# Moving one of two running sums of the first layer's modulation from VectorE to ScalarE and GpSimd

## The chip, the cores and the metric

The kernel runs on one core of a Trainium2 chip. The metric is the device time of one execution in microseconds (us), lower is better. Engines are called as in the profile: PE (TensorE matmul), PEld (its weight load), DVE (VectorE), ACT (ScalarE), POOL (GpSimd), SP (SyncE, which issues most of the DMAs).

## What is computed

The reference is a two-layer transformer block stack in fp32 on 256 tokens `x` and 256 context tokens `ctx`, width 1024. Each layer begins with a modulation that is made from two conditioning vectors, one for `x` and one for `ctx`:

```
mod_x = silu(c)     @ w_mod[l] + b_mod[l]     # 6 x 1024 columns
mod_c = silu(c_ctx) @ w_mod[l] + b_mod[l]
sh1, sc1, g1, sh2, sc2, g2 = split(mod, 6)
h = rmsnorm(x) * (1 + sc1) + sh1;   x = x + g1 * token_mixer(h)
h = rmsnorm(x) * (1 + sc2) + sh2;   x = x + g2 * channel_mixer(h)
```

The token mixer is a Fourier mix beside a gated linear attention; the channel mixer is a SwiGLU in layer 0 and eight experts with top-2 routing in layer 1. In layer 0 both token sets are carried, so each modulation is needed twice.

## The kernel before

fp32 products are made from high and low parts: a weight unit of 128x1024 is loaded on SP's queue (`load_unit`, L128), ACT writes its rounded high part (L145), DVE subtracts to get the low part (L149), and PE adds three products (`mm3`, L156 to L158). A unit's four `raw` places, three `hi` and three `lo` places come free when its readers are done. Stages follow one another: first modulation on PE, mixer of layer 0 (about 30 to 205 us), its output projection (to about 265 us), SwiGLU (to about 645 us), mixer of layer 1, experts.

The first two of the six modulation parts are made on PE at the start. The other four, for layer 0 (`g_mod(0, 1, 2)`, `s_mod(0, 1, 2)`, `g_mod(0, 2, 2)`), and all that follow for layer 1, run as side work in the function `mod_chunk` (L402): 512 columns at a time. A chunk has four loads of 256 rows of `w_mod` into a ring of three places (L128, `ring="mraw"`), and for each of its eight blocks of 128 rows one DVE instruction per conditioning vector (L419): `acc[x] = w * cs[x] + acc[x]`, 128x512 fp32. `x` is 0 for `c` and 1 for `c_ctx`. Each `acc` is first zeroed on POOL (L409) and gets `b_mod` in its first row by a small DMA on ACT's queue (L410). At the end of a chunk PE sums over the partitions with a matrix of ones: as rows (L425, copied by ACT, L426) or as columns (L429, copied by DVE, L431). The columns become `ac` (L360), which the normalised tokens are scaled by (L305 to L310).

A planner puts the instructions of each engine in order ahead of the run, by priority; every engine and every DMA queue then works strictly in that order. The L419 instructions stand inside `with later(LATER)`, which puts their priority 250 steps back: they fill room that the planner saw on DVE. The loads, the PE sums and the zeroing are not put back. Side work is pulled on by the main loops, one step for one or two weight units (`pull(mods, 1)`).

In the mixer DVE also runs the gated attention's levels (`widen`, L579 to L584, and the masked copies L642); the score matmuls (L598) and the PE sums L425 and L429 take their PSUM banks from one ring of four, tag `sc`.

Of the kernel before, what the change touches and what calls it, by code (L numbers as in the profile page):

```python
# [15 lines left out]
AF = mybir.ActivationFunctionType  # L16
OP = mybir.AluOpType
# [54 lines left out]
def hybrid_kernel(ctx: ExitStack, tc: tile.TileContext, a: dict, out: bass.AP, dbg=None, upto="end"):  # L72
    nc = tc.nc
# [18 lines left out]
    def spot(i, n=1):  # L92
        return spots[i // 4][:, i % 4:i % 4 + n, :].rearrange("p a b -> p (a b)")
# [27 lines left out]
    def load_unit(src, shape, ring="raw", queue=None):  # L121
        n = shape[0] * shape[1]
        if ring == "mraw":
            raw = spot(2 * (turn["mraw"] % 3), 2)[:, :n]
            turn["mraw"] += 1
        else:
            raw = place_of("raw", n)
        ins = (queue or nc.sync).dma_start(raw.rearrange("p (a b) -> p a b", a=shape[0]), src).ins  # L128
        if queue:
            return raw, shape  # L130
        behind(ins, W.get("load"))
        W["unit"] = ins
        if chained():
            W["load"] = ins
        return raw, shape
# [16 lines left out]
    def wsrc(w2d, r0, nb, c0, cols):  # L152
        return w2d[r0:r0 + nb * 128, c0:c0 + cols].rearrange("(k p) c -> p k c", p=128)
# [75 lines left out]
    cs = consts.tile([128, 16], F32, name="cs")  # L229
# [7 lines left out]
    def small(shape):  # L237
        return ps0.tile([128, 512], F32, name="sc", tag="sc", bufs=4)
# [164 lines left out]
    def mod_chunk(l, col, n_src, rows_out=None, cols_out=None):  # L403


        accs = []
        for x in range(n_src):
            acc = spot(10 + x)
            nc.gpsimd.memset(acc, 0.0)  # L409
            nc.scalar.dma_start(acc[0:1, :], a["b_mod"][l:l + 1, col:col + 512])  # L410
            accs.append(acc)
        for q in range(4):
            raw, _ = load_unit(wsrc(a["w_mod"][l], q * 256, 2, col, 512), (2, 512), ring="mraw")
            rv = raw.rearrange("p (a b) -> p a b", a=2)
            for k in range(2):
                kb = q * 2 + k
                for x in range(n_src):
                    with later(LATER):
                        nc.vector.scalar_tensor_tensor(accs[x], rv[:, k, :], cs[:, x * 8 + kb:x * 8 + kb + 1],  # L419
                                                       accs[x], op0=OP.mult, op1=OP.add)  # L420
            yield
        for x in range(n_src):
            ps = small([128, 512])
            if rows_out is not None:
                nc.tensor.matmul(ps, ones, accs[x], start=True, stop=True)  # L425
                nc.scalar.activation(rows_out[x], ps, AF.Copy)  # L426
            else:
                for j in range(4):
                    nc.tensor.matmul(ps[:, j:j + 1], accs[x][:, j * 128:(j + 1) * 128], ones[:, 0:1],  # L429
                                     start=True, stop=True)  # L430
                nc.vector.tensor_copy(cols_out[x], ps[:, 0:4])  # L431
# [3 lines left out]
    def g_mod(l, which, n_src):  # L435
        col = (2 if which == 1 else 5) * D
        if (l, which) == (1, 2):

            for hh in range(2):
                yield from mod_chunk(l, col + hh * 512, n_src, cols_out=[gcol[:, hh * 4:(hh + 1) * 4]])  # L440
            return
        gp[l, which] = [hbp.tile([128, D], F32, name="g", tag="g1", bufs=1) if l else spot(6 + 2 * x, 2)
                        for x in range(n_src)]
        for hh in range(2):
            yield from mod_chunk(l, col + hh * 512, n_src,
                                 rows_out=[g[:, hh * 512:(hh + 1) * 512] for g in gp[l, which]])

    def s_mod(l, which, n_src):
        mc = modp.tile([128, 2, 16], F32, name="modc", tag="modc", bufs=2)
        modc[l, which] = mc  # L450
        for ch in range(4):
            yield from mod_chunk(l, (0 if which == 0 else 3) * D + ch * 512, n_src,
                                 cols_out=[mc[:, x, ch * 4:(ch + 1) * 4] for x in range(n_src)])
# [845 lines left out]
    for turn_ in range(2):  # L1299
        for eng in range(2):  # L1300
            for j in range(4):
                k4 = turn_ ^ eng
                kb = 4 * k4 + j
# [507 lines left out]
```

## Time and profile before

| | us |
|---|---|
| median of 3 runs | 1665.8 |
| lowest, highest | 1665.4, 1669.24 |
| the profiled execution | 1667.27 |
| its span, first to last instruction | 1665.5 |

The profiled execution's time is 1.77 us above its span and 1.5 us above the median of the runs. In the profile, a row of a timeline or of the chain of waits begins with the start and the length in us; a group row gives a line, an engine, an operation, what is written and read, the count, the busy time and the mean length in ns. Rows that merge several instructions count them as x2, x3.

### The profile page before, as it was taken

To read this page: it belongs to the slowest core of one execution; us is meant where nothing else is said; L and a number is where in the kernel's file an instruction comes from. 1 tells how busy PE (TensorE), PEld (TensorE's weight loads), DVE (VectorE), ACT (ScalarE), POOL (GpSimd) and SP (SyncE) were. 2 spreads that over 40 slices of the span, in tenths; PEclk is the share of its full clock that TensorE was granted. 3 is DMA by queue.
4 is the path that set the end of the run, shared out by engine and by line. 5 is a ranking of instruction groups with operands and counts; after the bars stand their busy time and mean duration, and the time that the engine had idled before them with its cause. 6 is when DMAs were issued, how large, how long until landed. Compare 5 with 4: busy or idle time off the path is not lost.

```text
span 1665.5 us, 21562 instructions
## 1 busy us (share of the span) xinstructions
PE 1606.3 (96%) x8150; PEld 1159.5 (70%) x8150; DVE 1046.6 (63%) x1314; ACT 726.1 (44%) x892; POOL 27.5 (2%) x54
## 2 busy tenths in 40 slices
PE   7989999999999999999999999999999999999995
PEld 3868888788888888877786357874478844578532
DVE  3798897888567656866995127862178820588322
ACT  4733455322321347554775036741267611567201
POOL 1000000000000000000000000000000000000000
PEclk9999999999999999999999999999999999999997
DMA  9534385565666544546999999999999999999995
GB/s 372 160 102 136 96 267 163 163 189 171 189 190 201 156 128 140 174 154 240 332 357 318 415 406 413 407 406 407 409 412 409 410 390 408 410 414 406 384 405 201
DMA packets 186586, 479.06 MB, mean 288 GB/s; under 512 B 11585, under 2 KB 64961, under 8 KB 171873
## 3 DMA queue, kind: packets, MB, share of 16 engines
q1 hardware_dynamic: 185040, 473.80, 77.1%
q10 hardware_dynamic: 1074, 2.72, 0.5%
q8 instruction: 68, 1.11, 0.3%
q0 software_dynamic: 352, 1.00, 0.2%
q14 instruction: 52, 0.43, 0.1%
HBM read 476.43 MB, written 1.05 MB: 287 GB/s over the span
## 4 chain that ended last, share of the span: by engine, by line
PE 83%; DMA 6%; DVE 6%; ACT 3%; issue 1%; SPq 1%; DVEq 0%; ACTq 0%
PE h L1591 11%; PE mm L156 8%; PE mm L157 8%; PE mm L158 8%; PE h L1600 6%; PE h L1603 6%; PE h L1599 6%; PE y L156 5%; PE y L157 5%; PE y L158 5%; PE y L1623 4%; DMA rr<-moe_w 3%; PE sc L598 1%; PE sc L1570 1%; DVE lo L149 1%
## 5 line engine op out<-in xcount | busy, mean ns | idle before, releaser
L145 ACT ACTIVATE hi<-raw 128x1024 fp32r<-128x1024 f32 x127 | 134.6, 1059 | 303.2 <-PE mm L157 100.3
L177 DVE TENSOR_TENSOR rb<-raw,rb 128x2048 fp32r<-128x2048 f32 x73 | 167.1, 2290 | 80.2 <-ACT rb L177 60.5
L149 DVE TENSOR_TENSOR lo<-raw,hi 128x1024 fp32r<-128x1024 f32 x127 | 155.2, 1223 | 80.3 <-ACT hi L145 78.9
L419 DVE SCALAR_TENSOR_TENSOR rr<-rr,cs,rr 128x512 f32<-128x512 f32 x256 | 181.9, 747 | 9.6 <-DMA rr<-b_mod 4.6
L1600 PE MATMUL h<-rb,hg 128*128 128x512 f32 x448 | 177.2, 396 | 4.5 <-DVE rb L177 4.4
L156 PE MATMUL mm<-hbk,hi 128*128 128x512 f32 (+1 forms) x456 | 166.5, 366 | 1.1 <-DVE tm L837 1.0
L157 PE MATMUL mm<-hbk,hi 128*128 128x512 f32 (+1 forms) x456 | 163.6, 359 | 0.5 <-DVE hbk L310 0.5
L158 PE MATMUL mm<-hbk,lo 128*128 128x512 f32 (+1 forms) x456 | 163.8, 359 | 0.0
L177 ACT ACTIVATE rb<-raw 128x2048 fp32r<-128x2048 f32 x73 | 139.9, 1917 | 51.0 <-PE h L1603 31.8
L1591 PE MATMUL h<-raw,hgs 128*64 128x512 f32 (+1 forms) x720 | 143.4, 528 | 0.0
L177 DVE TENSOR_TENSOR sil<-sil,h 128x512 f32<-128x512 f32 (+1 forms) x44 | 29.1, 662 | 165.7 <-PE h L1591 148.5
L1599 PE MATMUL h<-rb,hg 128*128 128x512 f32 x288 | 109.1, 399 | 1.4 <-ACT rb L177 1.4
L1591 PEld LDWEIGHTS h<-raw,hgs 128*64 128x64 f32 x720 | 51.6, 137 | 77.5 <-issue 69.3
L1600 PEld LDWEIGHTS h<-rb,hg 128*128 128x128 f32 x448 | 85.1, 190 | 26.7 <-DVE rb L177 6.9
L177 DVE TENSOR_TENSOR rb<-raw,part 128x2048 fp32r<-128x2048 f32 x42 | 96.1, 2288 | 10.1 <-PE h L1600 4.6
L156 PEld LDWEIGHTS mm<-hbk,hi 128*128 128x128 f32 x456 | 85.9, 189 | 16.6 <-issue 2.7
L177 DVE TENSOR_TENSOR rb<-rr,rb 128x2048 fp32r<-128x2048 f32 x35 | 80.0, 2288 | 27.7 <-ACT rb L177 24.1
L177 ACT ACTIVATE part<-raw 128x2048 fp32r<-128x2048 f32 x42 | 80.4, 1914 | 36.2 <-DMA raw<-moe_w 16.8
L157 PEld LDWEIGHTS mm<-hbk,hi 128*128 128x128 f32 x456 | 86.0, 189 | 14.1 <-issue 1.0
L158 PEld LDWEIGHTS mm<-hbk,lo 128*128 128x128 f32 x456 | 86.0, 189 | 13.0
L1603 PE MATMUL h<-rb,hg 128*128 128x512 f32 x288 | 88.6, 393 | 2.5 <-DVE hg L177 2.5
L157 PE MATMUL y<-rb,ht 128*128 128x512 f32 x224 | 87.6, 391 | 0.0
(381 smaller groups left out, 2967.9 us busy)
## 6 DMA issues: line engine op xcount, KB each, us to landing
raw<-moe_w SPq DMA_DIRECT2D x212, 1024.0 KB
rr<-moe_w SPq DMA_DIRECT2D x110, 1024.0 KB
rr<-w_mod SPq DMA_DIRECT2D x80, 512.0 KB
raw<-ffn_w SPq DMA_DIRECT2D x72, 512.0 KB
raw<-w_in SPq DMA_DIRECT2D x32, 512.0 KB
raw<-w_out SPq DMA_DIRECT2D x23, 512.0 KB
raw<-moe_w SPq DMA_DIRECT2D x12, 512.0 KB
rb<-w_mod SPq DMA_DIRECT2D x5, 1024.0 KB
```

What stands on the lines that cost most here:

```text
L145: ins = nc.scalar.activation(hi, raw, AF.Copy).ins
L149: nc.vector.tensor_tensor(lo, raw, hi.bitcast(F32), op=OP.subtract)
L156: nc.tensor.matmul(ps, lh, rh, start=start, stop=False)
L157: nc.tensor.matmul(ps, lh, rl, start=False, stop=False)
L158: nc.tensor.matmul(ps, ll, rh, start=False, stop=stop)
L177: r = getattr(self.engine, name)(*args, **kw)
L419: nc.vector.scalar_tensor_tensor(accs[x], rv[:, k, :], cs[:, x * 8 + kb:x * 8 + kb + 1], accs[x], op0=OP.mult, op1=OP.add)
L1591: nc.tensor.matmul(H[i][0][x * 64:x * 64 + 64, :n], HG[e][:, k0 + j, :], hi[:, j, x * n:(x + 1) * n], start=(k0 + j == 0), stop=(k0 + j == 7))
L1599: nc.tensor.matmul(H[i][b], hgh[:, kb, :], hi[:, j, bc], start=(kb == 0), stop=False)
L1600: nc.tensor.matmul(H[i][b], hgh[:, kb, :], lo[:, j, bc], start=False, stop=False)
L1603: nc.tensor.matmul(H[i][b], hgl[:, kb, :], hi[:, j, bc], start=False, stop=(kb == 7))
L1623: nc.tensor.matmul(Y[e][0][hh * 64:hh * 64 + 64], ht[:, j0 + j, half], hi[:, j, xc], start=on, stop=off)
```

## The change

In layer 0's chunks of `mod_chunk`, the sum for `x = 1` is made in two steps on other engines: ACT multiplies the weight block in place by the column `cs` (an ACTIVATE Copy with a scale), and POOL adds it to the sum. The sum for `x = 0` stays on DVE, and so do all sums of layer 1. Both new instructions are under the same `later(LATER)`.

```diff
@@ -415,9 +415,14 @@
             for k in range(2):
                 kb = q * 2 + k
                 for x in range(n_src):
+                    c_ = cs[:, x * 8 + kb:x * 8 + kb + 1]
                     with later(LATER):
-                        nc.vector.scalar_tensor_tensor(accs[x], rv[:, k, :], cs[:, x * 8 + kb:x * 8 + kb + 1],
-                                                       accs[x], op0=OP.mult, op1=OP.add)
+                        if x and l == 0:
+
+                            nc.scalar.activation(rv[:, k, :], rv[:, k, :], AF.Copy, scale=c_)
+                            nc.gpsimd.tensor_tensor(accs[x], accs[x], rv[:, k, :], op=OP.add)
+                        else:
+                            nc.vector.scalar_tensor_tensor(accs[x], rv[:, k, :], c_, accs[x], op0=OP.mult, op1=OP.add)
             yield
         for x in range(n_src):
             ps = small([128, 512])
```

## Rows read from the trace of the kernel before

**Rows 1.** The page: span, busy time by engine, the span in 40 slices.
```profile
span 1665.5 us, 21562 instructions
PE 1606.3 (96%) x8150; PEld 1159.5 (70%) x8150; DVE 1046.6 (63%) x1314; ACT 726.1 (44%) x892; POOL 27.5 (2%) x54
...
PE   7989999999999999999999999999999999999995
...
DMA  9534385565666544546999999999999999999995
```

**Rows 2.** Stages of 25 us: busy time of each engine, with the sum.
```profile
100.00:125.00 25.00, 20.64 (x153) 16.34 (x152) 24.97 (x42) 8.25 (x13) 0.00 (x0) 1.00 0.44 128
125.00:150.00 25.00, 25.00 (x163) 19.73 (x162) 24.23 (x42) 11.53 (x14) 1.05 (x2) 1.00 0.34 105
...
250.00:275.00 25.00, 23.40 (x177) 21.94 (x176) 23.95 (x49) 15.58 (x34) 0.00 (x0) 1.00 0.54 156
275.00:300.00 25.00, 25.00 (x110) 20.06 (x110) 13.42 (x18) 9.24 (x14) 1.05 (x2) 1.00 0.49 139
...
sum 275.00, PE 268.30 PEld 220.88 DVE 232.28 ACT 129.07 POOL 9.78; mean PE 24.39 PEld 20.08 DVE 21.12 ACT 11.73 POOL 0.89
```

**Rows 3.** The chain of waits, 93 to 125 us: start, length, what.
```profile
101.28 1.36 DVE rr L419 x3
...
110.54 0.73 DVE rr L419 x2
...
121.28 3.41 issue
124.70 1.96 PE sc L425 x4
```

**Rows 4.** DVE in order of time, places where the sums run.
```profile
43.72 0.75 DVE L419 SCALAR_TENSOR_TENSOR rr<-rr,cs,rr 128x512 f32<-128x512 f32 x1
...
101.16 2.73 DVE L419 SCALAR_TENSOR_TENSOR rr<-rr,cs,rr 128x512 f32<-128x512 f32 x4
...
110.42 2.07 DVE L419 SCALAR_TENSOR_TENSOR rr<-rr,cs,rr 128x512 f32<-128x512 f32 x3
...
118.78 2.84 DVE L419 SCALAR_TENSOR_TENSOR rr<-rr,cs,rr 128x512 f32<-128x512 f32 x4
...
123.87 0.72 DVE L642 COPY_PREDICATED A<-masks,sc 128x512 f32<-128x512 uint8 x1
...
263.14 3.40 DVE L419 SCALAR_TENSOR_TENSOR rr<-rr,cs,rr 128x512 f32<-128x512 f32 x5
```

**Rows 5.** POOL's groups, whole span.
```profile
L409 POOL MEMSET rr<- 128x512 f32 x32 | 16.8, 525 | 536.2 <-PE mm L425 98.5 <-DVE sil L1029 98.1 <-PE mm L429 80.4
...
L1731 POOL TENSOR_TENSOR res<-macc,raw 128x512 f32<-128x512 f32 x2 | 2.5, 1271 | 893.2 <-DVE macc L177 892.5 <-DVE rn L267 0.7
```

**Rows 6.** POOL's copies at L471 (minimum, median, maximum ns), and DVE beside them.
```profile
L471 POOL COPY rr<-rr x8: 290/294/846, 27.9 to 580.4; 128x128 f32<-128x128 f32 x8
...
27.92 1.00 POOL L471 COPY rr<-rr 128x128 f32<-128x128 f32 x4 [11.48 <-DMA rr<-w_in]
...
577.94 2.32 DVE L419 SCALAR_TENSOR_TENSOR rr<-rr,cs,rr 128x512 f32<-128x512 f32 x3
...
578.51 2.14 POOL L471 COPY rr<-rr 128x128 f32<-128x128 f32 x4 [7.69 <-issue]
```

**Rows 7.** DVE's groups from 100 to 150 us.
```profile
L419 DVE SCALAR_TENSOR_TENSOR rr<-rr,cs,rr 128x512 f32<-128x512 f32 x25 | 17.2, 745 | 0.1
L642 DVE COPY_PREDICATED A<-masks,sc 128x512 f32<-128x512 uint8 x22 | 16.0, 732 | 0.0
```

**Rows 8.** ACT, an SBUF to SBUF copy of 128x512 at L475.
```profile
L475 ACT ACTIVATE rr<-rr x2: 614/624/633, 580.3 to 580.9; 128x512 fp32r<-128x512 f32 x2
```

**Rows 9.** DVE in order of time, the last sum of four later chunks.
```profile
152.26 1.41 DVE L419 SCALAR_TENSOR_TENSOR rr<-rr,cs,rr 128x512 f32<-128x512 f32 x2
...
175.79 0.74 DVE L419 SCALAR_TENSOR_TENSOR rr<-rr,cs,rr 128x512 f32<-128x512 f32 x1
...
205.79 0.74 DVE L419 SCALAR_TENSOR_TENSOR rr<-rr,cs,rr 128x512 f32<-128x512 f32 x1
...
236.85 0.75 DVE L419 SCALAR_TENSOR_TENSOR rr<-rr,cs,rr 128x512 f32<-128x512 f32 x1
```

**Rows 10.** The chain of waits around the PE sums of the same four chunks.
```profile
154.16 1.68 PE sc L429 x16
...
177.76 1.68 PE sc L429 x16
...
207.21 0.79 PE sc L429 x8
...
238.86 0.79 PE sc L429 x8
```

**Rows 11.** Who waited for whom: SP's queue from 20 to 330 us, then ACT up to 700 us.
```profile
SPq L128 <- DVE rr L419: 116.9, 30, 13.4
...
ACT hi L145 <- PE mm L157: 100.3, 29, 4.8
...
ACT hi L145 <- DMA raw<-ffn_w: 4.1, 1, 4.1
```

**Rows 12.** The page: DVE's groups for weight splits and attention levels, L419 among them.
```profile
L149 DVE TENSOR_TENSOR lo<-raw,hi 128x1024 fp32r<-128x1024 f32 x127 | 155.2, 1223 | 80.3 <-ACT hi L145 78.9
L419 DVE SCALAR_TENSOR_TENSOR rr<-rr,cs,rr 128x512 f32<-128x512 f32 x256 | 181.9, 747 | 9.6 <-DMA rr<-b_mod 4.6
```

## The prediction

> **What bounds the kernel now.** I read the page first: PE is busy in 1606.3 of 1665.5 us and DVE in 63% [rows 1]. That is an average, so I went to the stages in which nearly all of the changed instructions run, from 50 to 325 us, cut in pieces of 25 us. There PE is busy for 268.30 of 275 us [rows 2], so it waits 6.70 us. This is the first thing to see: whatever DVE is spared, PE can't get back more than those 6.70 us, and some 0.7 us before 50 us, because PE's own work does not change. The second thing is where they lie: 4.36 us (25.00 - 20.64) between 100 and 125 us, where DVE is busy for 24.97 of 25 us, and 1.60 us between 250 and 275 us, where DVE has 23.95 [rows 2]. From 275 to 300 us DVE has 13.42 and PE does not wait at all [rows 2]: there a lighter DVE is worth nothing. The chain of waits agrees: through the first of these places it runs on DVE, L419 in it, and then shows 3.41 us before the PE sum L425 [rows 3]. What lies behind 325 us is full of PE and, in its second half, of DMA [rows 1]; it begins when the stages before it end, so I pass a gain or a loss on to the end one to one.
>
> **The change, part by part.** Layer 0 has eight chunks here (two, four and two of `g_mod`, `s_mod`, `g_mod`) with eight blocks each: 64 L419 leave DVE, 64 ACT copies and 64 POOL additions come.
>
> *What DVE is spared.* Four L419 in a row take 2.73 us, three take 2.07 us [rows 4]: 0.66 us more for each one more. So DVE is spared 64 x 0.66 = 42 us, nearly all beside PE work that goes on anyway. On the path I count three places. Between 101 and 122 us there are 4 + 3 + 4 = 11 L419 [rows 4]; half of them are for x = 1, so the L642 that ends at about 124.5 us comes 5.5 x 0.66 = 3.6 us sooner. PE's wait of 3.41 us ends at 124.70 [rows 3], while the sums it reads ended at 118.78 + 2.84 = 121.6 us [rows 4]. The profile does not name what it waited for; its bank comes from the ring which L642 empties, and it starts 0.1 us after that L642, so I take it as waiting for this and as moving with it. The five L419 at 263.14 us hold up the token blocks that PE wants next [rows 4]: 2.5 x 0.66 = 1.6 us, of which I take 1.0, since the 1.60 us of waiting lie partly elsewhere in that stretch. One more, at 43.72 us [rows 4], lies between the normalisations of the first two tiles of x, which PE waits for: 0.7 us. Sum: -5.3 us, bounds 0 and -7.4 (all of PE's waiting).
>
> *What POOL's additions cost DVE.* The same form of addition, 128x512 and both inputs in SBUF, takes 1.271 us on POOL at the end of the kernel [rows 5], when DVE does next to nothing. Beside a busy DVE the trace has only copies: alone 290 ns each; at 578.5 us, while DVE runs L419, two of the four take up to 846 ns, and DVE's three L419 take 2.32 us in place of 2.07 [rows 4, 6]. So each held the other up: a copy waited 0.56 us for DVE (846 - 290; the four took 2.14 us in place of 1.00), and DVE lost 0.25 us to two copies, 0.125 us each. That copy reads 128 elements a partition, the addition 2 x 512, eight times as many: an estimate of 8 x 0.125 = 1.0 us of DVE for an addition that meets a DVE instruction with SBUF inputs. The bounds are 0 (it meets none, or slips in between) and the 1.271 us that it lasts; I take 1.0, as the copies are the nearest row with a busy DVE. That is more than the 0.66 us which the addition spares. In the three places above there are 5.5 + 2.5 + 1 = 9 additions. Not all meet such an instruction: from 100 to 150 us L642, which reads PSUM, has 16.0 of 49.2 us of DVE [rows 2, 7], so I count 0.7 of them: 9 x 1.0 x 0.7 = +6.3 us, bounds 0 and 9 x 1.271 = +11.4. Elsewhere DVE has 275 - 232.28 = 42.7 us of idle time [rows 2] for a net 0.04 us (0.7 x 1.0 - 0.66) an addition: free.
>
> The Trainium skill, page "SBUF — State Buffer", section "SBUF: two separate sides", speaks against this change: the port pair that DVE and GpSimd share is an exclusive lock, held for the whole instruction, and a DVE instruction with two SBUF inputs needs it against a GpSimd instruction that reads SBUF. The waiting of the copies agrees; the 0.125 us that DVE lost is less than a whole copy (290 ns). By that rule the sum above would be +11.4 at most, for 1.271 us an addition; it is the third rival.
>
> *The new chain in front of the PE sums.* x = 1's sum is now ready after DVE's x = 0 instruction (the scaling writes over what that reads, so it must wait for it), one ACT copy (0.624 us [rows 8]) and one addition (1.271 us, and 0.56 us of waiting as the copies had): 0.62 + 1.27 + 0.56 = 2.45 us after it, where before it was 0.66 us: 1.8 us later. If the last two additions queue up, 1.83 us more. PE takes its instructions in order, so a sum that is late holds all of PE. The slack before runs from the end of a chunk's last L419 to the x = 1 half of its PE sums [rows 9, 10]: 154.16 + 0.84 - (152.26 + 1.41) = 1.3 us, 177.76 + 0.84 - 176.53 = 2.1, 207.21 - 206.53 = 0.7 and 238.86 - 237.60 = 1.3. Against 1.8 us that is 0.5 + 0 + 1.1 + 0.5 = +2.1 us; with the queue 0.5 + 1.83 and so on, 2.3 + 1.6 + 2.9 + 2.3 = +9.1; 0 if the planner puts these sums further back. Of the other four chunks one has 124.70 - 121.6 = 3.1 us [rows 3, 4], and three lie where DVE has room; I count none of them. I take +2.1.
>
> *ACT, SP and the zeroing.* ACT gets 64 x 0.624 = 40 us, with 129.07 of 275 busy [rows 2]. A copy that waits for a late L419 holds the splits L145 queued behind it; those mostly wait for PE anyhow (100.3 us in 29 waits against L157 alone, [rows 11]): nothing, and some 2 us for a unit if that cover is gone. SP's loads wait 30 times for L419 to free a place [rows 11]; now for an addition up to 1.8 us later, and weights are queued behind them. ACT's splits waited once for a landing, 4.1 us [rows 11]: I take nothing, and up to 1.8 us a unit if loads become late. POOL's zeroing (0.525 us [rows 5]) and the small DMA on ACT's queue behind it can now wait for one addition, under the same cover.
>
> Sum: -5.3 + 6.3 + 2.1 = +3.1 us on the profiled execution, 1667.27 + 3.1 = 1670.4. That execution is 1.5 us above the median, so against the runs: 1665.8 + 3.1 = 1668.9, say **1669 us**.
>
> **The rivals.** *Faster: additions slip in between.* POOL reads while DVE runs L642 or small instructions and DVE loses next to nothing. Then the second and third term fall away: 1665.8 - 5.3 = 1660.5, down to 1658.4 at PE's bound. For it: DVE lost only 0.125 us to a copy. Against it: DVE lost those 0.25 us to copies that read an eighth as much.
>
> *Slower: PE waits for POOL at the ends of chunks.* Place: L425 and L429 in PE's order, whose position the planner chose for an addition with no one in its way. Price: +9.1 us in place of +2.1 in the third term: 1665.8 - 5.3 + 6.3 + 9.1 = 1675.9. It decides from the point where the last addition ends over 1.3 us after the place that x = 0's own sum would be taken. For it: slacks of 0.7 to 2.0 us. Against it: the one long wait before such a sum was not for its data [rows 3, 4].
>
> *Slower: each addition holds DVE for its whole length.* A mechanism of this kernel: 1.271 us against 0.66 spared, in every one of the 9 places. 1665.8 - 5.3 + 11.4 + 2.1 = 1674.0. For it: the two copies at 846 ns. Against it: DVE's loss was less than half of a copy.
>
> *It does nothing.* The planner fills DVE's spared room with the next chunk's L419, which run earlier, and the full stretches stay full: 1666.
>
> **How the numbers follow.** A measurement of this kernel can tell about 0.3%, 5 us, from no change. The forecast, which lies within that, has 0.42, "nothing" 0.04, the faster rival 0.14, PE's waiting 0.20, the whole-length hold 0.20. So faster 0.14, same 0.46, slower 0.40. The range goes from 1659 (the faster rival but for its end) to 1665.8 - 5.3 + 11.4 + 9.1 = 1681, with something for delayed loads 1682.
>
> **What would show it.** In the changed profile: POOL has 64 more TENSOR_TENSOR, with a mean well above 1.271 us if DVE holds them up; L419 and L149 have means above 0.747 and 1.223 us [rows 12], or gaps before them, if POOL holds DVE up; PE's busy share from 100 to 125 us rises above 20.64 if DVE was the bound there; waits of PE before L425 and L429 that end with POOL show the third term. The prediction is wrong if PE waits for splits (ACT stuck behind a scaling) or for loads, or if the stages after 325 us, which I left alone, come in another order.

## The result: 45.8 us slower, and the profile after

The changed kernel takes 1711.42 us (median of 4 runs, 1709.82 to 1713.65) against 1665.6 us before in the same comparison: a ratio of 1.0266, 95% interval 1.0253 to 1.0279. The forecast was 1669 us with a range up to 1682 us, so it was wrong, in size above all: a loss fifteen times the 3.1 us of its sum.

In the changed file what stood behind L419 is five lines further down: DVE's sum is L425, the scaling on ACT L422, the addition on POOL L423, the PE sums L430 and L434, the attention levels L584, L586 and L589, their masked copies L647 and the copies for the scores L641.

The page of the changed kernel; compare [rows 1]:

```profile
span 1710.1 us, 21716 instructions
...
PE 1624.7 (95%) x8150; PEld 1172.5 (69%) x8150; DVE 1057.2 (62%) x1250; ACT 767.4 (45%) x956; POOL 132.0 (8%) x118
...
PEclk9999989999999999999999999999999999999998
```

DVE has 64 instructions fewer and yet is busy 10.6 us longer (1057.2 - 1046.6). That is the first sign: the 42 us it was spared have been taken back with more. PE does the same 8150 matmuls in 18.4 us more, the sign of a slower clock. Span less busy time, it stands idle for 85.4 us (1710.1 - 1624.7) where it was 59.2 us (1665.5 - 1606.3): 26.2 us more. The two make up the 44.6 us by which the span has grown.

The stages of 25 us in which the change stands; compare [rows 2]:

```profile
100.00:125.00 25.00, 20.72 (x125) 16.52 (x125) 24.86 (x27) 10.70 (x18) 13.63 (x8) 0.86 0.42 126
125.00:150.00 25.00, 23.34 (x161) 18.19 (x158) 23.49 (x32) 12.03 (x18) 9.17 (x7) 1.00 0.24 67
150.00:175.00 25.00, 22.65 (x128) 18.74 (x127) 18.59 (x28) 11.77 (x15) 5.57 (x5) 0.86 0.37 125
...
225.00:250.00 25.00, 17.10 (x75) 14.02 (x74) 12.42 (x16) 6.79 (x11) 5.03 (x5) 0.78 0.44 139
...
325.00:350.00 25.00, 25.00 (x108) 20.03 (x107) 14.50 (x15) 10.59 (x15) 6.20 (x6) 1.00 0.45 124
```

Three of these stages before the change:

```profile
150.00:175.00 25.00, 25.00 (x160) 21.12 (x159) 20.48 (x32) 8.26 (x13) 1.05 (x2) 1.00 0.58 170
225.00:250.00 25.00, 24.91 (x126) 20.73 (x125) 23.11 (x45) 14.84 (x29) 1.05 (x2) 1.00 0.72 228
325.00:350.00 25.00, 25.00 (x120) 20.94 (x119) 19.72 (x29) 6.48 (x8) 1.05 (x2) 1.00 0.56 172
```

From 125 to 150 us DVE does 32 instructions where it did 42, and is busy for nearly as long as before: on average each has become longer. The granted clock (the first number behind POOL's, 1.00 at full speed) falls below 1 in stage after stage, where before it was 1.00 in every stage from 50 to 400 us. From 325 us on PE is busy throughout, as before: the loss arises while layer 0's chunks run, and passes on to the end.

DVE in order of time, in the stage where before it was full, and POOL beside it:

```profile
103.59 1.66 DVE L425 SCALAR_TENSOR_TENSOR rr<-rr,cs,rr 128x512 f32<-128x512 f32 x1
105.18 2.32 DVE L149 TENSOR_TENSOR lo<-raw,hi 128x1024 fp32r<-128x1024 f32 x1
107.42 1.77 DVE L584 TENSOR_TENSOR ch<-ch,eb 128x512 f32<-128x512 f32 x1
109.11 1.75 DVE L586 TENSOR_TENSOR ch<-ch,eb 128x512 f32<-128x512 f32 x1
110.78 0.71 DVE L647 COPY_PREDICATED A<-masks,sc 128x512 f32<-128x512 uint8 x1
...
112.55 0.67 DVE L584 TENSOR_TENSOR ch<-ch,eb 128x512 f32<-128x512 f32 x1
...
99.50 10.82 POOL L423 TENSOR_TENSOR rr<-rr,rr 128x512 f32<-128x512 f32 x6 [2.62 <-ACT rr L422]
```

This is the mechanism in one view. While POOL's six additions run (99.5 to 110.3 us), the DVE instructions with two SBUF inputs that start in that time are 0.9 to 1.1 us longer: the sum L425 has 1.66 us against 0.75, the split L149 2.32 us against 1.22, L584 1.77 us; as soon as the additions are over the same L584 has 0.67 us. L647, which has one input in PSUM and one in SBUF, keeps its 0.71 us. The additions take turns with DVE and are longer themselves:

```profile
L423 POOL TENSOR_TENSOR rr<-rr,rr 128x512 f32<-128x512 f32 x64 | 104.4, 1632 | 99.2 <-ACT rr L422 54.6 <-issue 31.6 <-DMA rr<-b_mod 5.5
```

1.632 us in the mean, where the same form alone has 1.271 [rows 5].

PE at the largest wait of the changed kernel, and the granted clock over seven stretches that I picked by it, with their sum:

```profile
236.06 0.39 PE L158 MATMUL mm<-hi,rb 128*128 128x512 f32 x1
236.29 0.39 PE L156 MATMUL mm<-hi,rb 128*128 128x512 f32 x1
244.58 1.84 PE L434 MATMUL sc<-sqc,rr 128*128 128x1 f32 x8 [7.90 <-issue]
...
247.28 0.63 PE L156 MATMUL mm<-hi,rb 128*128 128x512 f32 x1
247.71 0.63 PE L157 MATMUL mm<-lo,rb 128*128 128x512 f32 x1
...
239.20:249.40 10.20, 4.82 (x15) 4.19 (x16) 2.97 (x5) 0.60 (x1) 0.53 (x1) 0.51 0.28 103
...
sum 44.20, PE 36.40 PEld 31.47 DVE 29.65 ACT 11.77 POOL 10.70; mean PE 5.20 PEld 4.50 DVE 4.24 ACT 1.68 POOL 1.53
```

PE stands for 7.90 us before the sum L434. Then it runs on at half speed: one matmul each 0.43 us (247.28 to 247.71) against 0.23 us before the wait (236.06 to 236.29), the granted clock 0.51, that is 1.2 GHz of 2.4. In all there are 44.2 us at that level in this part of the kernel, with PE busy for 36.4 of them.

### The profile page after: what moved, and what is told of

Read it like the earlier page. It is cut to its first block, busy times and chain, and to the rows that moved or that the text cites. A ratio compares the mean times of both kernels' runs of the same rounds, so it can differ in the third digit from the quotient of the medians.

```text
span 1710.1 us, 21716 instructions
## 1 busy us (share of the span) xinstructions
PE 1624.7 (95%) x8150; PEld 1172.5 (69%) x8150; DVE 1057.2 (62%) x1250; ACT 767.4 (45%) x956; POOL 132.0 (8%) x118
## 3 DMA queue, kind: packets, MB, share of 16 engines
q8 instruction: 68, 1.11, 0.3%
## 4 chain that ended last, share of the span: by engine, by line
PE 72%; DMA 4%; DVE 3%; ACT 2%; issue 1%; SPq 0%; DVEq 0%; ACTq 0%
PE h L1596 10%; PE mm L156 6%; PE h L1605 6%; PE h L1608 6%; PE mm L157 6%; PE h L1604 6%; PE mm L158 6%; PE y L156 5%; PE y L157 5%; PE y L158 5%; PE y L1628 4%; DMA rr<-moe_w 3%; PE sc L1575 1%; PE sc L1397 1%; PE mm L434 1%
## 5 line engine op out<-in xcount | busy, mean ns | idle before, releaser
L149 DVE TENSOR_TENSOR lo<-raw,hi 128x1024 fp32r<-128x1024 f32 x127 | 162.3, 1278 | 83.6 <-ACT hi L145 82.5
L425 DVE SCALAR_TENSOR_TENSOR rr<-rr,cs,rr 128x512 f32<-128x512 f32 x192 | 163.6, 871 | 17.6 <-DMA rr<-w_mod 7.9
L423 POOL TENSOR_TENSOR rr<-rr,rr 128x512 f32<-128x512 f32 x64 | 104.4, 1632 | 99.2 <-ACT rr L422 54.6
```

The source lines that it names most:

```text
L149: nc.vector.tensor_tensor(lo, raw, hi.bitcast(F32), op=OP.subtract)
L423: nc.gpsimd.tensor_tensor(accs[x], accs[x], rv[:, k, :], op=OP.add)
L425: nc.vector.scalar_tensor_tensor(accs[x], rv[:, k, :], c_, accs[x], op0=OP.mult, op1=OP.add)
```

## The experiments

Theory A: POOL's additions come late and hold DVE. Theory B: ACT's queue stands behind scalings that wait for DVE. Theory C: the planner's other order is what costs. Five of the runs tell them apart. Four runs (nothing, no scaling, zeroing, copies) leave out a part of the sums and serve for their time alone. All medians below are beside runs of the kernel before on the same chip (1666.9, 1667.9 and 1668.1 us for the three sets); ratios have 95% intervals.

**Nothing in the place of DVE's sums.**

```diff
                         if x and l == 0:
-                            nc.scalar.activation(rv[:, k, :], rv[:, k, :], AF.Copy, scale=c_)
-                            nc.gpsimd.tensor_tensor(accs[x], accs[x], rv[:, k, :], op=OP.add)
+                            pass
```

> Leaves out layer 0's sums for x = 1 altogether (64 scalings and 64 additions; the zeroing, the bias and the PE sums stay). It shows what sparing DVE is worth with nothing put in its place. Theory A (the additions on POOL come late and hold DVE, ring places and loads come free late, PE waits at its sums and its clock falls) and theory B (ACT's queue stands behind scalings that wait for DVE) both expect PE's waits before 325 us mostly gone: 1660 us, 1658 to 1663. Theory C (the planner's other order is what costs, whatever engine does the work) expects it to stay well above before, over 1675 us.

Measured: 1660.54 us, ratio 0.996 (0.9946 to 0.9974), 6.3 us faster than before. Two stages of this run, compare [rows 2]:

```profile
100.00:125.00 25.00, 23.16 (x163) 17.88 (x162) 23.56 (x40) 10.22 (x16) 1.05 (x2) 1.00 0.33 106
250.00:275.00 25.00, 24.51 (x184) 23.04 (x183) 16.30 (x31) 15.49 (x31) 0.00 (x0) 1.00 0.30 88
```

PE gains 2.52 us (23.16 - 20.64) and 1.11 us (24.51 - 23.40) in the two stages that the forecast named. So the relief of DVE is worth about what the first term of the sum said (5.3 us), and that is a bound for whatever else is done with these sums. It speaks against theory C, but does not decide it, for the order of this run is not that of the changed kernel; the run with copies below has that order.

**The scaling on ACT, the addition on DVE.**

```diff
-                            nc.gpsimd.tensor_tensor(accs[x], accs[x], rv[:, k, :], op=OP.add)
+                            nc.vector.tensor_tensor(accs[x], accs[x], rv[:, k, :], op=OP.add)
```

> ACT scales in place as in the change, but DVE adds (TENSOR_TENSOR, 0.69 us where the old instruction took 0.66): POOL has no part. Theory A expects 1664 to 1672 us, as DVE's load is that of before and no addition is late. Theory B expects the loss to stay, 1695 to 1712 us, since every scaling still waits for DVE in ACT's queue.

Measured: 1670.95 us, ratio 1.0022 (1.0012 to 1.0032). The scalings, and ACT's waiting for DVE, cost some 4 us (DVE is busy for 1044.8 us, as before the change). Theory B explains a small part.

**POOL's additions without the scaling.**

```diff
-                            nc.scalar.activation(rv[:, k, :], rv[:, k, :], AF.Copy, scale=c_)
```

> Leaves out the 64 scalings on ACT: POOL adds the raw weight block. Theory A expects most of the loss to stay, 1690 to 1711 us, the additions being the same. Theory B expects most of it gone, 1663 to 1680 us.

Measured: 1709.6 us, ratio 1.024 (1.0217 to 1.0262). Without any part of ACT 42.7 us of the 45.8 are there. Theory A stands, and it has two halves: POOL is late, or POOL holds DVE.

**POOL as long busy, but reading nothing.**

```diff
-                            nc.gpsimd.tensor_tensor(accs[x], accs[x], rv[:, k, :], op=OP.add)
+                            nc.gpsimd.memset(rv[:, k, :], 0.0)
+                            nc.gpsimd.memset(rv[:, k, :], 0.0)
+                            nc.gpsimd.memset(accs[x], 0.0)
```

> In place of each addition POOL zeroes the weight block twice and the sum once (3 x 0.525 = 1.57 us, near the 1.63 us that an addition took in the changed kernel), behind the same scaling: POOL is as long busy and frees a ring place as late, but reads nothing of SBUF. The sums for x = 1 are left out by it. If holding DVE is what costs within theory A: 1664 to 1675 us, and DVE's weight splits back at 1.22 us. If the lateness of POOL alone (its own 1.6 us, behind ACT) costs: 1695 to 1712 us.

Measured: 1670.01 us, ratio 1.0018 (1.0009 to 1.0028). POOL is busy for 3 x 34 us, near the 104.4 us of the additions, though it is through with a ring place after two of the three zeroings; the loss is 3.1 us in place of 45.8. The level instruction in this run, by its shortest, middle and longest time:

```profile
L588 DVE TENSOR_TENSOR ch<-ch,eb x16: 416/683/704, 84.8 to 180.8; 128x512 f32<-128x512 f32 x14, 128x256 f32<-128x256 f32 x2
```

Its longest time is 704 ns, that of a DVE left alone; the longest split L149 has 1.228 us and the longest sum for x = 0 0.754 us. So zeroing holds none of the DVE instructions with two SBUF inputs, and reading does. It is not without effect on DVE, though: the normalisation L962 (L955 before), a TENSOR_SCALAR with one data input, in SBUF, has 0.755 us at most before and here, beside zeroings, up to 1.617 us:

```profile
L962 DVE TENSOR_SCALAR xn<-resid,rsy x6: 744/753/1617, 243.1 to 633.3; 128x1024 f32<-128x1024 f32 x6
```

There are few of these: by the working shown further down, the lengthening of all DVE instructions in this run is some 1.3 us, against 48.5 us in the changed kernel. What the lateness of POOL costs without holds can be read here too: against the run with nothing in the place, 1670.0 - 1660.5 = 9.5 us, the scaling included.

**Half the reading.**

```diff
-                            nc.gpsimd.tensor_tensor(accs[x], accs[x], rv[:, k, :], op=OP.add)
+                            nc.gpsimd.tensor_copy(accs[x], rv[:, k, :])
```

> POOL copies the scaled block into the sum in place of adding it: it reads 512 elements a partition and not 2 x 512. The sums for x = 1 are left out by it. If the cost is DVE held for as long as POOL reads, a held instruction is longer by some 0.55 us and not 1.1, DVE gets less than it is spared, and most of the loss goes: 1664 to 1680 us. If each meeting costs the same whatever is read: 1695 to 1712 us.

Measured: 1676.67 us, ratio 1.0056 (1.004 to 1.0073). The same instruction as above, now with copies on POOL, and then in the changed kernel with additions:

```profile
L586 DVE TENSOR_TENSOR ch<-ch,eb x16: 415/683/1099, 86.0 to 185.3; 128x512 f32<-128x512 f32 x14, 128x256 f32<-128x256 f32 x2
```

```profile
L586 DVE TENSOR_TENSOR ch<-ch,eb x16: 416/684/1772, 92.4 to 202.8; 128x512 f32<-128x512 f32 x14, 128x256 f32<-128x256 f32 x2
```

A held instruction has 1.099 us with copies that read 512 elements a partition and 1.772 us with additions that read 2 x 512, against 0.704 us: it loses 0.4 us or 1.07 us. The hold goes with what POOL reads. And the loss does not fall in proportion: with holds of 0.4 us, shorter than the 0.66 us that are spared, it is 8.7 us in place of 45.8.

This run also decides on theory C. In the traces of the changed kernel and of this run DVE (407 instructions in the changed kernel's first 400 us), ACT (349), PE (1925 matmuls) and SP (the first 60 loads) go through the same instructions in the same order; only POOL's 64 instructions differ. So 37 us of the loss (45.8 - 8.7) come from these and not from the order. The copies are also shorter (0.966 us in the mean against 1.632), so POOL is less late with them; the run with zeroing limits that part to 9.5 us.

**The scaled block in a scratch tile.**

```diff
-                            nc.scalar.activation(rv[:, k, :], rv[:, k, :], AF.Copy, scale=c_)
-                            nc.gpsimd.tensor_tensor(accs[x], accs[x], rv[:, k, :], op=OP.add)
+                            part = spot(13 + 2 * k)
+                            nc.scalar.activation(part, rv[:, k, :], AF.Copy, scale=c_)
+                            nc.gpsimd.tensor_tensor(accs[x], accs[x], part, op=OP.add)
```

> ACT writes the scaled block into one of two scratch tiles and not in place, POOL adds from there: the scaling no longer waits for DVE's x = 0 instruction, and a ring place comes free without POOL. (The scratch is the zeroed gate tile, which is zeroed anew for layer 1.) POOL's reads stay. If holding DVE by POOL's reads is what costs, the loss stays: 1690 to 1712 us. If late ring places and the loads queued behind them on SP carry it: 1665 to 1680 us.

Measured: 1705.64 us, ratio 1.0233 (1.0216 to 1.025). Freeing the ring places without POOL gives back 6 us by the medians, or 8 us with each kernel against its own runs before (45.8 and 37.7 us). In the changed kernel SP does wait for POOL where it had waited for DVE, compare [rows 11]:

```profile
SPq L128 <- POOL rr L423: 132.9, 31, 15.5
```

but 132.9 us in 31 waits are not much over the 116.9 us in 30 of before. In this run SP waits as long for DVE again, and most of the loss stays without POOL in that place:

```profile
SPq L128 <- DVE rr L426: 134.0, 33, 16.5
```

**The PE sums put back.**

```diff
+        if l == 0:
+            tc.cur_priority += 2 * LATER
         for x in range(n_src):
             ps = small([128, 512])
...
+        if l == 0:
+            tc.cur_priority -= 2 * LATER
```

> The changed kernel with layer 0's PE sums put back by a further 500 steps of priority, so that PE comes to them later. If PE's waits right before these sums (8.07, 4.03 and 1.6 us in the changed kernel, and the slow clock after each) carry the loss: 1675 to 1690 us. If DVE's splits and attention levels are late themselves: 1695 to 1712 us.

Measured: 1724.41 us, ratio 1.034 (1.031 to 1.0369), worse than the change itself and outside both ranges expected. PE's order differs widely in this run (872 of the first 1800 matmuls stand where they stood), so it says less than I wanted: only that asking for these sums later did not help. Why it cost more was not shown.

**The last two chunks alone, and the first six alone.**

```diff
-                        if x and l == 0:
+                        if x and l == 0 and col >= 5 * D:
```

(and `col < 5 * D` for the first six)

> The change for the last two of layer 0's eight chunks alone (the second gate, in the SwiGLU stage, where PE does not wait and DVE has room). If the loss needs a full DVE: 1663 to 1669 us, and POOL's additions there with a mean under 1.6 us. If each addition costs the same wherever it is, 16 of 64 cost a quarter of the loss: 1675 to 1680 us.

> The change for the first six of layer 0's eight chunks alone. Together with the run of the last two (+6.6 us) it shows whether the losses add: 1700 to 1706 us if they do. If the six alone cost the whole, 1709 to 1714 us.

Measured: 1674.52 us, ratio 1.0041 (1.0027 to 1.0055), for the last two; 1705.55 us, ratio 1.0228 (1.0207 to 1.0249), for the first six. They add: 6.6 + 37.5 = 44.1 us. The last two cost 6.6 us, between the two ranges expected, and more than a stage with room should; the stages of that run tell why:

```profile
250.00:275.00 25.00, 18.96 (x117) 17.11 (x117) 22.64 (x37) 17.48 (x36) 13.89 (x8) 0.90 0.51 149
275.00:300.00 25.00, 25.00 (x143) 22.36 (x142) 11.96 (x18) 11.30 (x20) 0.00 (x0) 0.96 0.40 112
300.00:325.00 25.00, 25.00 (x108) 19.84 (x107) 19.46 (x17) 13.13 (x19) 14.52 (x10) 1.00 0.51 151
```

The first of the two chunks runs from 250 to 275 us, in the last part of the output projection, where DVE was full, and there PE falls from 23.40 us [rows 2] to 18.96. The second runs from 300 to 325 us with POOL busy for as long, and PE does not wait at all, although the eight additions there meet DVE as well (13.93 us in all, 1.74 us each, against 1.27 alone). In these two stages an addition costs nothing where DVE has room, and much where it has none.

**More work on DVE instead.** The kernel before with one instruction more behind each x = 1 sum of layer 0:

```diff
+                        if x and l == 0:
+                            nc.vector.tensor_tensor(rv[:, k, 0:256], rv[:, k, 0:256], rv[:, k, 256:512], op=OP.add)
```

> The kernel before, with 64 more DVE instructions: behind each of layer 0's sums for x = 1 one addition of 128x256 (0.42 us, 0.34 us more in a row) in the weight block that is done with, at the same low priority. DVE gets 64 x 0.34 = 22 us more work, more than it had to bear in the changed kernel on balance (48 us of being held less 42 us spared). If DVE's total time is what costs: 1700 us and more. If it matters which instructions are late (the holds fall on splits and attention levels, and the planner does not know of them): 1667 to 1685 us.

Measured: 1682.73 us, ratio 1.0079 (1.0052 to 1.0105). 22 us more on DVE at low priority cost 14.6 us. So room on DVE in these stages is scarce even for work that can be put anywhere: the 42 us it could be spared are worth 6.3 us, 22 us on top cost 14.6. But it takes more than DVE's time to explain the change, whose balance for DVE is only some 6 us (48.5 - 42, below; 10.6 us on the page) and whose loss is three times as large.

## Why the prediction was wrong, point by point

**What DVE is spared** was right: forecast -5.3 us with a bound of -7.4 us, measured -6.3 us with nothing in its place. The two stages named gave back 3.6 us of it (2.52 + 1.11); the third place, at 43.72 us, was not looked at by itself.

**What an addition costs DVE** was right in size: forecast 1.0 us where it meets an instruction with SBUF inputs, by scaling up the 0.125 us of the copies; measured 1.07 us. That it came so near is in part luck: the copy of 512 elements cost 0.4 us, where the same scaling gives 0.5. The share of 0.7 was near as well. Taking each kind of DVE instruction's mean from 40 to 366 us of the changed kernel less its mean before, times its count, the sum is 48.5 us: 0.76 us for each of 64 additions, forecast 0.7. Three of its groups:

```profile
L425 DVE SCALAR_TENSOR_TENSOR rr<-rr,cs,rr 128x512 f32<-128x512 f32 x65 | 72.2, 1111 | 11.3 <-DMA rr<-w_mod 7.9 <-issue 1.0 <-POOL rr L409 0.7
L149 DVE TENSOR_TENSOR lo<-raw,hi 128x1024 fp32r<-128x1024 f32 x42 | 58.2, 1389 | 22.4 <-ACT hi L145 22.1
...
L584 DVE TENSOR_TENSOR ch<-ch,eb 128x512 f32<-128x512 f32 x14 | 13.9, 991 | 0.0
```

L425 has 1.111 us where L419 had 0.747, and L149 1.389 where it had 1.223 [rows 12]. The same working gives 10.7 us for the run with copies and 1.3 us for the one with zeroing.

**The step that failed** is the one after it: "Elsewhere DVE has 275 - 232.28 = 42.7 us of idle time [rows 2] for a net 0.04 us (0.7 x 1.0 - 0.66) an addition: free." I counted 9 of the 64 additions, those in the places where PE waited before, and let the idle time of 275 us pay for the other 55. From 6.3 us faster with nothing in the place to 45.8 us slower, the additions and scalings cost 52.1 us; the 9 were priced at 11.4 us at most, and what is not a hold costs 9.5 us by the run with zeroing. An estimate from these: some 31 us (52.1 - 11.4 - 9.5) came from the 55 that were called free. They were tried only by chunks, 37.5 us for the first six and 6.6 us for the last two. Two things were wrong in that step. A net figure hides where the holds fall. What is spared are L419, of low priority. Of the 48.5 us held, 23.7 us fall on the sums left on DVE (65 x (1.111 - 0.747)) and the rest mostly on splits, attention levels and others in front of PE; and as DVE keeps to the order planned without the holds, a hold on a sum delays what stands behind it too. One case is in the view of DVE above: four instructions in a row are held, L586 ends at 110.9 us, the copy L641 that waits for it comes after, and PE waits for that:

```profile
111.66 0.49 PE L603 MATMUL sc<-ch,km 64*128 64x128 f32 x2 [3.26 <-ACT km L641]
```

And idle time summed over 275 us is no reserve for a hold that falls in a full stretch: in the run with the last two chunks PE lost nothing to eight additions from 300 to 325 us, and 4.44 us (23.40 - 18.96) in the stage from 250 to 275 us, with eight of them. A gain was capped by PE's waiting before, 6.70 us, as the forecast said; a loss had no such cap, and its upper bound, +11.4 us, was taken from the same 9 places.

**The chain in front of the PE sums** was forecast as +2.1, up to +9.1 us. Zeroing in place of additions, as late and without reading, costs 9.5 us over nothing; some 4 us of that are the scaling's by the second run, which leaves an estimate of some 5 us, within the bounds. With holds the waits are longer, 7.90 us at one sum alone. What the sum L434 waited for there was not POOL's addition but the DVE sum for x = 0, which had waited 5.97 us for a load of `w_mod`, and that for a ring place on SP's queue. SP issued that load at 233.73 us, as soon as POOL's addition out of the place had ended (232.39 + 1.31 = 233.70 us): it is the wait of 15.5 us in SP's row above, and the path that the forecast named under ACT, SP and zeroing and priced at nothing.

```profile
232.39 1.31 POOL L423 TENSOR_TENSOR rr<-rr,rr 128x512 f32<-128x512 f32 x1
...
242.94 1.54 DVE L425 SCALAR_TENSOR_TENSOR rr<-rr,cs,rr 128x512 f32<-128x512 f32 x2 [5.97 <-DMA rr<-w_mod]
```

**ACT, SP and the zeroing** at nothing: the scaling costs some 4 us (1670.95 against 1666.87 us with the addition on DVE), freeing the places without POOL brings 6 to 8 us.

**A term that was missing** is TensorE's clock. In the changed kernel the six waits of PE from 2.2 to 7.9 us between 40 and 366 us each run into a stretch at 1.2 GHz; a seventh stretch stands behind shorter waits. It is not always so: behind the wait of 3.41 us before the change [rows 3] the clock stayed at 1.00 [rows 2]. With a pitch of 0.43 for 0.23 us, the 36.4 us of busy PE in the slow stretches could have been 36.4 x 0.23 / 0.43 = 19.5 us: up to 17 us of the loss by these rows, near the 18.4 us that PE is busy longer on the page. It was not tried apart from the waits that go before it, so its share stays an estimate.

**The rivals.** The third, each addition holding DVE for its whole length, named the right mechanism; its price (1674 us) was made with the same 9 places and fell with them. The second, PE waiting at the ends of chunks, happens, but with all of the lateness and the scaling it costs 9.5 us without holds, a fifth of the loss. The rule of the Trainium skill in "SBUF — State Buffer", section "SBUF: two separate sides", that spoke against the change was right on what is held: DVE instructions with two SBUF inputs are held by POOL's reads and not by its zeroing, and L647 with one SBUF input is not held, as it says. The hold measured is 1.07 us of an addition that has 1.27 alone, a little less than the whole instruction.

No version came out that beats the kernel before: the bound with these sums left out is 6.3 us, and every way tried of making them elsewhere costs more than it gives.

## What to carry to other kernels

Before work goes from VectorE to GpSimd, compare what the move spares VectorE for one instruction (0.66 us here) with what GpSimd's reading holds it (1.07 us for two inputs of 512 fp32, 0.4 us for one). With the additions, whose hold is longer than what is spared, the move lost 45.8 us. A shorter hold was not enough either: with copies it still lost 8.7 us, and with zeroing, which reads nothing, 3.1 us; the lateness of the moved work and the scaling on ScalarE have a price too. Price each hold at the most urgent instruction that it can fall on, stage by stage: idle time elsewhere did not pay for it here. Where PE is the bound, the gain of a relief ends at PE's present waits, while a loss has no such end, and the new long waits here cost PE stretches at half its clock as well.

## What the runs showed of the hardware that was not expected

- POOL's reads hold a DVE instruction with two SBUF inputs for a time that goes with the elements read: 0.125 us for 128, 0.4 us for 512, 1.07 us for 2 x 512 a partition. Zeroing on POOL, 192 times 0.53 us beside a busy DVE, held none of these (L588 704 ns at most), but lengthened a TENSOR_SCALAR of 128x1024 with one SBUF data input from 0.755 to 1.617 us.
- The turns go both ways: four DVE instructions in a row were held while additions ran, and the six additions in that time took 10.82 us in place of 7.6 (6 x 1.271).
- PE's six waits of 2.2 to 7.9 us each ran into a stretch with a granted clock of 0.51; with a seventh behind shorter waits these stretches are 44.2 us, where before the change every stage from 50 to 400 us shows 1.00, also the one behind a wait of 3.41 us.
